# An RWKV-7, attention and expert encoder: the triangular inverse starts on its matrices, output products come in halves, opening rows go to ScalarE

## The chip, the cores and the metric

The kernel runs as one program on one core of a Trainium2 chip. The time is the device time of one execution in microseconds (us). A core has TensorE (PE; its weight loads are listed apart as PEld), VectorE (DVE), ScalarE (ACT), GpSimd (POOL) and SyncE (SP), which here only issues DMAs. Each engine works through its own instructions in order and waits on semaphores for the others.

## What is computed

One batch of 256 tokens with 1024 channels goes through two layers. Layer 0 mixes tokens with a bidirectional RWKV-7 recurrence, layer 1 with dilated window attention; behind each stands a mixture of 32 experts, of which every token takes two. The reference, cut to the part in which the change lies:

```python
for i in range(DEPTH):                       # DEPTH = 2
    mod = silu_c @ ada_w[i] + ada_b[i]       # six rows of 1024: shift, scale, gate, twice
    sh_t, sc_t, ga_t, sh_c, sc_c, ga_c = jnp.split(mod, N_MOD, axis=-1)
    hn = modulate(rms_norm(x, norm_tm_g[i]), sh_t, sc_t)
    tm = rwkv7_mix(hn, ...) if i % 2 == 0 else dilated_attention_mix(hn, ...)
    x = x + ga_t[:, None, :] * tm
    x = x + ga_c[:, None, :] * hier_moe(modulate(rms_norm(x, norm_cm_g[i]), sh_c, sc_c), ...)

def step(state, inp):                        # in rwkv7_mix, per head of 64, forwards and backwards
    sa = jnp.einsum('bhvk,bhk->bhv', state, a_t)
    state = state * w_t[:, :, None, :] + sa[:, :, :, None] * b_t[:, :, None, :] \
            + v_t[:, :, :, None] * k_t[:, :, None, :]
    y_t = jnp.einsum('bhvk,bhk->bhv', state, r_t)
# then: y normalised per head, gated by g, summed over both directions, and o @ w_o
```

## The kernel before, in words

The program has four stages, each of which needs the whole result of the one before: RWKV mixing, experts of layer 0, attention, experts of layer 1. The change touches the first alone.

**The opening.** `ada_rows` (line 402) forms the scale and shift rows of layer 0. For m = 1, then m = 0, 16 products with `silu` as weights (tile `row` in PSUM, two banks of 512 columns) add up over the eight slices of `w_ada`, which land in the ring `aring`. Each bank is copied to SBUF (`row[0]` by ScalarE, line 420; `row[1]` by VectorE, line 421), and eight products with the column `four` (tile `ada`) turn the 1024 values into eight columns; `ada_columns` (line 367) adds the bias and leaves them in `modc`. `scales` (line 481) and `modulated` (lines 674 to 684) use them on `xk`, `xr`, `xw`, `xa` and `xv`, of which `xk` feeds the first key products, tile `kr`.

**Eight pairs of heads.** Each pair i runs through four generators. `project` forms keys (`kr`), values (`v`), norms (`ss`, `vc`) and rates (`L`). `ready` (scale_keys, then chunks) scales the keys, forms the products `G`, masks them into `GV` and `GI` (line 927), casts the matrix to 16 bits (`Ah` on ScalarE at line 938, the rest `Al` on GpSimd at 939, minus the identity at 940), and goes on to the transposes `BT`, the products `R2` and the bonus `sT`; it then notes ("ready", i). `inverse` inverts the triangular matrix by doubling: each level is a round of small products (tile `iv`), an eviction `T` and `X` by ScalarE (line 999) and a masked `Q` by VectorE (line 1021); it ends with `TT` (line 1053). `recur` steps through four chunks (`U`, `S`, `Y`, `R1`), each step a product, an eviction and the next product. `finish` normalises the pair's output (`gvar` at line 1147, a reciprocal root of nine small VectorE instructions, `YT` at 1158), transposes it (`yT`) and gates it (`gT`).

**The order.** `weave` (line 277) writes the instructions of all generators into one order before anything runs: a generator yields a delay or a condition, a clock of estimated PE time (`pe_work`) decides whose turn it is, and `RANK` breaks ties. TensorE keeps this order as written; the other engines take theirs from the priorities that `weave` sets. Beside the pairs, `modulation_flow` adds up the other modulation rows on VectorE (line 376, tile `acc`) and ends each with eight products of one column (`ada<-cst,acc`), read by `modc` at line 367. `outputs` multiplies finished pairs with the output weights: `out_first` (pairs 0 to 3) and `out_second` (pairs 4 to 7), in blocks of 512 columns (tile `wo`). The last four blocks (pair 7) come behind the weave, then the router.

The condition that holds the inverse back before the change, and the one on its stream:

```python
            yield after(("ready", i))      # inverse, line 1005
            yield 1.0
                yield after(("ready", i))  # inverses, line 1303
```

Of the kernel before, what the change touches and what calls it, by code (L numbers as in the profile page):

```python
# [14 lines left out]
AF = mybir.ActivationFunctionType  # L15
# [219 lines left out]
def trunk(ctx, tc, names, aps, out, stages=("rwkv", "moe0", "attn", "moe1"), dbg=None, ring=2):  # L235
# [12 lines left out]
    def bank(name="ps", tag="ps"):  # L248
        return psum[-1][tag].tile([128, 512], F32, name=name, tag=tag)
# [11 lines left out]
    def on_pe(i):  # L261

        return tc.keep_in_program_order(i) if pinned[0] else i

    def mm(o, lhsT, rhs, start=True, stop=True, **kw):
        n = int(np.prod(rhs.shape[1:]))
        t = 2 * max(0.1, n / 1200) if rhs.dtype == F32 else max(0.03, n / 2400)
        if lhsT.shape[0] <= 64 or int(np.prod(lhsT.shape[1:])) <= 64:
            t /= 2
        pe_work[0] += t  # L270
        return on_pe(nc.tensor.matmul(out=o, lhsT=lhsT, rhs=rhs, start=start, stop=stop, **kw))  # L271
# [31 lines left out]
    V, A, P = nc.vector, nc.scalar, nc.gpsimd  # L303
# [98 lines left out]
    def ada_rows(tags, places, pool):  # L402


        four = pool.tile([128, 1], F32, name="four")
        V.tensor_reduce(out=four, in_=IDENT[:, 0:128:32], axis=AX.X, op=ALU.add)
        pc = bank(name="ada", tag=tags[4])
        for n, m in enumerate((1, 0)):
            ps = [bank(name="row", tag=t) for t in tags[2 * n:2 * n + 2]]
            for q in range(2):  # L410
                ws = modulations.take(*[(0, m, 4 * q + g) for g in range(4)])
                if modulations.issued >= len(ADA_FIRST):
                    stream.fill()
                for e in range(2):
                    for g in range(4):
                        k = 4 * q + g
                        mm(ps[e][32 * g:32 * g + 32, :], silu[:, k:k + 1].to_broadcast([128, 32]),
                           ws[g][:, e * 512:(e + 1) * 512], start=(q == 0), stop=(q == 1), skip_group_check=True)
            row = [p.tile([128, 512], F32, name="row", tag=t) for p, t in places[2 * n:2 * n + 2]]
            A.activation(out=row[0], in_=ps[0], func=AF.Copy)  # L420
            V.tensor_copy(out=row[1], in_=ps[1])
            for c in range(8):
                mm(pc[:, 8 * m + c:8 * m + c + 1], row[c // 4][:, c % 4 * 128:(c % 4 + 1) * 128], four)
            ada_columns(0, m, pc[:, 8 * m:8 * m + 8])
# [182 lines left out]
    def rwkv(pool):  # L607
# [137 lines left out]
        done = set()  # L745

        def after(*what):
            return lambda: all(w in done for w in what if w[1] >= 0)
# [165 lines left out]
        def chunks(i, w):  # L914

            AR, BK = w["AR"], w["BK"]
            GI = turns(i, [128, 2, 2, 4, 64], "GI")
            GV = sup.tile([128, 2, 2, 4, 64], F32, name="GV", bufs=1)
            aq = "p (a q) n -> p a q n"
            for z in range(2):  # L920
                pair = [bank(name="G") for _ in range(2)]
                for c in range(4):
                    for hh, ps in enumerate(pair):
                        mm(ps[:, c * 128:(c + 1) * 128], BK[half(hh), z, c, :], AR[half(hh), z, c, :])
                for hh, ps in enumerate(pair):
                    for o, t in ((0, GV), (64, GI)):
                        V.tensor_tensor(out=t[:, z, hh].rearrange(aq, q=2),
                                        in0=ps.rearrange("p (a q n) -> p a q n", a=2, q=2)[:, :, :, o:o + 64],
                                        in1=mk[:, z, :, o:o + 64].unsqueeze(1).to_broadcast([128, 2, 2, 64]),
                                        op=ALU.mult)  # L930
                yield 1.6

            gv = GV.rearrange("p z h c n -> p (z h) c n")
            Ah, Al = A16[2 * (i % 2):2 * (i % 2) + 2]
            for q in range(2):
                a = gv[half(q), :, 1 - q::2, :]
                h, l = (t.rearrange("p (g a) m -> p g a m", a=2)[half(q)] for t in (Ah, Al))
                A.copy(out=h, in_=a)
                P.tensor_tensor(out=l, in0=a, in1=h, op=ALU.subtract)
            V.tensor_tensor(out=Ah, in0=Ah, in1=N16.unsqueeze(1).to_broadcast([128, 8, 64]), op=ALU.add)  # L940
            if i == 0:
                yield lambda: "hidden_gate" in done
            BT = turns(i, [128, 2, 2, 2, 128], "BT")
            for par in range(2):
                ps = bank(name="BT")
                for z in range(2):
                    for a in range(2):
                        o = (z * 2 + a) * 128
                        tr(ps[:, o:o + 128], BK[:, z, 2 * a + par, :])
                A.activation(out=BT[:, par].rearrange("p z a n -> p (z a n)"), in_=ps, func=AF.Copy,  # L950
                             scale=sgn[:, par:par + 1])
                yield 0.1
            if i == 0:
                yield lambda: ("project", 0) in done
            vc = w["vc"]

            UV = turns(i, [128, 2, 4, 128], "UV")
            for z in range(2):
                for par in range(2):
                    A.copy(out=UV[half(par), z, par::2, :], in_=vc[half(par)])  # L960
            yield 0.1
            R2 = turns(i, [128, 4, 2, 64], "R2")
            ps = bank(name="R2")
            for s in range(4):
                for hh in range(2):
                    o = (s * 2 + hh) * 64
                    for z in range(2):
                        c = step_of(z, s)
                        p = half(c % 2)
                        mm(ps[half(1 - c % 2), o:o + 64], GV[p, z, hh, c, :], vc[p, c // 2, hh * 64:hh * 64 + 64])  # L970
            A.activation(out=R2.rearrange("p s h n -> p (s h n)"), in_=ps, func=AF.Copy)
            w.update(GI=GI, BT=BT, R2=R2, UV=UV)
            bonus(i, w)
            done.add(("ready", i))

        def inverse(i, w):
# [25 lines left out]
            def square():  # L1002
                return bank(name="iv", tag="iv")

            yield after(("ready", i))
            yield 1.0
            Ah, Al = A16[2 * (i % 2):2 * (i % 2) + 2]

            X = tile16("X16")
# [3 lines left out]
            for l in range(1, 6):  # L1013
# [4 lines left out]
                ps = square()  # L1018
# [14 lines left out]
            ps = square()  # L1033
# [22 lines left out]

        def recur(i, w):

            yield after(("inverse", i), ("finish", i - 2))
            yield 0.9  # L1060
            AR, GI, BT, TT, R2, UV, WC = (w[n] for n in ("AR", "GI", "BT", "TT", "R2", "UV", "WC"))
            YT = w["YT"] = sub.tile([128, 2, 2, 128], F32, name="YT")
# [1 line left out]
            for s in range(4):  # L1064
# [3 lines left out]
                else:  # L1068
                    R = odd.tile([128, 2, 64], F32, name="R", bufs=2)
                    ps = bank(name="R1", tag="ch")  # L1070
# [5 lines left out]
                ps = bank(name="U", tag="ch")  # L1076
# [8 lines left out]
                if s < 3:  # L1085
# [5 lines left out]
                    for z, c in enumerate(cz):  # L1091
                        for h, n in hs:
                            mm(pS[h, z * 64:z * 64 + 64], BT[:, c % 2, z, c // 2, n], UV[:, z, c, n],
                               start=(s == 0 and z == 0), stop=True, skip_group_check=True)
# [10 lines left out]
                if s > 0:  # L1105
                    for z, h in enumerate(hs):
                        mm(py[h, 0:128], AR[:, z, cz[z], 64:128], ST[:, z, :], start=True, stop=False,
                           skip_group_check=True)
                for hh in range(2):
                    for z, h in enumerate(hs):  # L1110
                        w["last"] = mm(py[h, hh * 64:hh * 64 + 64], GI[:, z, hh, cz[z], :], UV[:, z, cz[z], hh * 64:hh * 64 + 64],
                                       start=(s == 0 and hh == 0), stop=True, skip_group_check=True)
# [119 lines left out]
        def block(ps, t, w, k, start, stop):  # L1232
            mm(ps, oT[:, k, t * 128:(t + 1) * 128], w[:, (k % 4) * 512:(k % 4 + 1) * 512], start=start, stop=stop)

        def out_first():

            yield after(("project", 7), ("finish", 3), ("gate", 2))
            for c in range(2):
                w = gated(stream.take(("rwo", 0, c)), gates[0, 2][:, c * 512:(c + 1) * 512], 4)
                yield 6.0  # L1240
                for t in range(NTT):
                    ps = bank(name="wo", tag="pp")
                    for k in range(4):
                        block(ps, t, w, k, k == 0, k == 3)
                        yield
                    add_out(ps, t, c)

        def out_second(po, ks, w):
            for k in ks:
                for n, (t, c) in enumerate(po):  # L1250
                    if k == 6 and n == 2:
                        yield after(("recur", 7))
                    mm(po[t, c], oT[:, k, t * 128:(t + 1) * 128], w[:, k % 2, c * 512:(c + 1) * 512],
                       start=(k == 4), stop=(k == 7))
                    yield

        po, oT = {}, None

# [41 lines left out]

        def inverses():
            for i in range(8):
                yield after(("ready", i))
                yield from inverse(i, ws[i])

        def recurrences():
            for i in range(8):
                yield after(("inverse", i))
                yield from recur(i, ws[i])

        def finishes():
# [787 lines left out]
```

## Time and profile before

| | us |
|---|---|
| median of three runs | 1184.85 (1182.29 to 1189.32) |
| the profiled execution | 1175.46 |
| its span, first to last instruction | 1173.7 |
| PE busy in the span | 1031.4 (88%) |
| DVE busy | 620.2 (53%) |
| ACT busy | 431.6 (37%) |

The profile is of one execution. Its page gives the busy time of each engine, the span in 40 slices with the clock that TensorE was granted, the chain of work that ended last, and the costliest groups. Behind the page, the trace can be asked for instructions in order of time, for busy times in chosen stretches, and for who waited for whom. A number in brackets behind an instruction is the time that its engine sat idle just before it, with what ended that.

### The profile page before, as it was taken

The page shows a single profiled execution, that of the slowest core. Times are in us where ns is not written, and L with a number is a line of the kernel's source. Part 1 is how long each engine was busy: PE and PEld are TensorE (multiplying, and loading weights), DVE is VectorE, ACT ScalarE, POOL GpSimd, SP SyncE. Part 2 cuts the span into 40 slices and gives each one's busy share as a digit, 9 for nine tenths or more (in the row PEclk, how much of TensorE's full clock was granted, in tenths as well). Part 3 has the DMA queues.
Part 4 walks back from the last instruction along what each step waited for, and adds up shares of the span by engine and source line. Part 5 has one row for each costly group of instructions (what it writes and reads, how often), then busy time and mean ns, then how long its engine had stood idle before and what let it go on. Part 6 is the DMA issues. An engine that isn't in the chain of part 4 may idle for free. (4 is left out here: it accounts for less than half of the span.)

```text
span 1173.7 us, 25024 instructions
## 1 busy us (share of the span) xinstructions
PE 1031.4 (88%) x10580; PEld 675.4 (58%) x10580; DVE 620.2 (53%) x1460; ACT 431.6 (37%) x913; POOL 149.7 (13%) x110
## 2 busy tenths in 40 slices
PE   7789889999988998978987899898979999789886
PEld 2666667766766555434442388687868754344422
DVE  4774678478585446212211367999984752121112
ACT  2544455455446342101000366656544621010012
POOL 1020010010012600000000012122472000000000
PEclk9789999899979999989998999999989999899999
DMA  9462524325243676998999987887745589999995
GB/s 366 179 237 77 181 77 151 109 95 168 74 131 129 269 288 251 388 418 358 421 420 421 420 358 266 310 303 275 282 145 171 209 339 409 413 370 421 420 422 234
DMA packets 53197, 322.01 MB, mean 274 GB/s; under 512 B 5922, under 2 KB 6562, under 8 KB 21458
## 3 DMA queue, kind: packets, MB, share of 16 engines
q1 hardware_dynamic: 51986, 315.88, 69.0%
q0 software_dynamic: 800, 3.36, 0.7%
q8 instruction: 87, 1.43, 0.5%
q10 hardware_dynamic: 288, 1.05, 0.3%
q14 instruction: 36, 0.29, 0.1%
HBM read 319.22 MB, written 1.05 MB: 273 GB/s over the span
## 5 line engine op out<-in xcount | busy, mean ns | idle before, releaser
L271 PE MATMUL gu<-wring,xT 128*32 128x512 f32 x1024 | 132.6, 616 | 16.8 <-PEq L1609 10.2
L376 DVE SCALAR_TENSOR_TENSOR acc<-aring,silu,acc 128x512 f32<-128x512 f32 x140 | 116.0, 860 | 17.5 <-DMA aring<-in_w_ada_dram 17.3
L467 POOL TENSOR_TENSOR wl<-wring,wh 128x1024 f16<-128x1024 f32 x24 | 57.0, 2377 | 403.4 <-ACT wh L466 400.9
L271 PE MATMUL qkv<-hh,wh 128*128 128x256 f16 x384 | 106.1, 276 | 1.8 <-ACT hh L1761 1.8
L271 PE MATMUL qkv<-hl,wh 128*128 128x256 f16 x384 | 105.7, 276 | 1.8 <-DVE hl L1762 1.8
L271 PE MATMUL qkv<-hh,wl 128*128 128x256 f16 x384 | 106.0, 276 | 1.2 <-DVE wl L473 1.2
L271 PEld LDWEIGHTS gu<-wring,xT 128*32 128x32 f32 x1024 | 30.8, 112 | 100.5 <-issue 82.0
L271 PEld LDWEIGHTS <-wh 128*128 128x128 f16 x768 | 76.1, 99 | 12.8 <-issue 3.5
L271 PE MATMUL dn<-wring,hidT 128*32 128x256 f32 x1024 | 65.5, 404 | 18.4 <-ACT hidT L1564 18.4
L473 DVE SCALAR_TENSOR_TENSOR wl<-wring,wh 128x1024 f16<-128x1024 f32 x56 | 70.5, 1264 | 16.4 <-ACT wh L469 16.3
L271 PE MATMUL acc<-y,back 128*128 128x512 f32 (+1 forms) x144 | 66.0, 581 | 10.3 <-DVE y L1591 8.1
L271 PEld LDWEIGHTS xT<-oh,x 128*128 128x128 f32 x512 | 59.0, 192 | 21.1 <-issue 9.2
L469 ACT ACTIVATE wh<-wring 128x1024 f16<-128x1024 f32 x56 | 58.6, 1050 | 33.0 <-PE qkv L271 23.2
L1366 DVE SCALAR_TENSOR_TENSOR sg<-sg,gu 128x256 f32<-128x256 f32 x16 | 6.7, 420 | 116.8 <-ACT sg L1365 116.8
L1591 DVE TENSOR_TENSOR y<-dn,ga 128x512 f32<-128x512 f32 x28 | 19.4, 692 | 88.3 <-PE dn L271 56.7
L271 PE MATMUL xT<-oh,x 128*128 128x128 f32 x512 | 63.5, 280 | 2.5 <-DVE oh L1475 2.5
L1365 ACT ACTIVATE sg<-gu 128x256 f32<-128x256 f32 x16 | 6.1, 384 | 145.6 <-PE gu L271 145.6
L271 PEld LDWEIGHTS dn<-wring,hidT 128*32 128x32 f32 x1024 | 31.9, 115 | 48.2 <-ACT hidT L1564 22.3
L1507 ACT ACTIVATE back<-bT 128x256 f32<-128x256 f32 x16 | 6.2, 386 | 131.0 <-PE acc L271 131.0
L271 PE MATMUL qkv<-wh,hh 128*128 128x256 f16 x192 | 52.3, 273 | 0.0
L271 PE MATMUL qkv<-wh,hl 128*128 128x256 f16 x192 | 52.3, 273 | 0.0
L271 PE MATMUL qkv<-wl,hh 128*128 128x256 f16 x192 | 52.3, 273 | 0.0
(355 smaller groups left out, 2090.4 us busy)
## 6 DMA issues: line engine op xcount, KB each, us to landing
wring<-in_w_moe_dram SPq DMA_DIRECT2D x192, 1024.0 KB, 19.8
aring<-in_w_ada_dram SPq DMA_DIRECT2D x96, 512.0 KB, 4.6
wring<-in_w_qkv_dram SPq DMA_DIRECT2D x36, 1024.0 KB, 8.4
wring<-in_w_kr_dram SPq DMA_DIRECT2D x8, 1024.0 KB, 5.9
wring<-in_w_vl_dram SPq DMA_DIRECT2D x8, 640.0 KB, 5.0
wring<-in_w_rwo_dram SPq DMA_DIRECT2D x4, 1024.0 KB, 8.1
wring<-in_w_ato_dram SPq DMA_DIRECT2D x4, 1024.0 KB, 6.6
x<-in_x_dram POOLq DMA_DIRECT2D x2, 512.0 KB, 7.2
```

The costliest lines, as they stand in the source:

```text
L271: return on_pe(nc.tensor.matmul(out=o, lhsT=lhsT, rhs=rhs, start=start, stop=stop, **kw))
L376: V.scalar_tensor_tensor(out=acc[:, s], in0=w[:, s], scalar=silu[:, k:k + 1], in1=acc[:, s], op0=ALU.mult, op1=ALU.add)
L467: eng.tensor_tensor(out=lo, in0=src, in1=hi, op=ALU.subtract)
L469: A.activation(out=hi, in_=src, func=AF.Copy, scale=by)
L473: V.scalar_tensor_tensor(out=lo, in0=src, scalar=by, in1=hi, op0=ALU.mult, op1=ALU.subtract)
L1365: A.activation(out=o, in_=ps[:, 0:256], func=AF.Tanh, scale=0.5)
L1366: V.scalar_tensor_tensor(out=o, in0=o, scalar=1.0, in1=ps[:, 0:256], op0=ALU.add, op1=ALU.mult)
L1507: A.activation(out=back, in_=ps[:, 0:S], func=AF.Copy)
L1591: V.tensor_tensor(out=y, in0=py[c], in1=gates[i, 5][:, c * 512:(c + 1) * 512], op=ALU.mult)
```

## The change

Three edits. First, `chunks` notes ("matrices", i) as soon as `Ah` is complete, and `inverse` waits for that in place of ("ready", i), then 4.0 of the planner's units in place of 1.0; `recur` now asks for ("ready", i) itself. Second, the output products are written as two products of 256 columns, with a yield behind each. Third, the second bank of the opening rows is copied by ScalarE.

```diff
@@ ada_rows
             A.activation(out=row[0], in_=ps[0], func=AF.Copy)
-            V.tensor_copy(out=row[1], in_=ps[1])
+            A.activation(out=row[1], in_=ps[1], func=AF.Copy)
@@ chunks
             V.tensor_tensor(out=Ah, in0=Ah, in1=N16.unsqueeze(1).to_broadcast([128, 8, 64]), op=ALU.add)
+            done.add(("matrices", i))
@@ inverse
-            yield after(("ready", i))
-            yield 1.0
+            yield after(("matrices", i))
+            yield 4.0
@@ recur
-            yield after(("inverse", i), ("finish", i - 2))
+            yield after(("inverse", i), ("ready", i), ("finish", i - 2))
@@ out_first
-                        block(ps, t, w, k, k == 0, k == 3)
-                        yield
+                        for e in range(2):
+                            o = slice(e * 256, e * 256 + 256)
+                            mm(ps[:, o], oT[:, k, t * 128:(t + 1) * 128], w[:, k * 512 + e * 256:k * 512 + e * 256 + 256],
+                               start=(k == 0 and e == 0), stop=(k == 3), skip_group_check=True)
+                            yield
@@ out_second
-                    mm(po[t, c], oT[:, k, t * 128:(t + 1) * 128], w[:, k % 2, c * 512:(c + 1) * 512],
-                       start=(k == 4), stop=(k == 7))
-                    yield
+                    for e in range(2):
+                        o = c * 512 + e * 256
+                        mm(po[t, c][:, e * 256:e * 256 + 256], oT[:, k, t * 128:(t + 1) * 128], w[:, k % 2, o:o + 256],
+                           start=(k == 4 and e == 0), stop=(k == 7), skip_group_check=True)
+                        yield
@@ inverses, recurrences
-                yield after(("ready", i))
+                yield after(("matrices", i))
-                yield after(("inverse", i))
+                yield after(("inverse", i), ("ready", i))
```

What this does to the order shows at three places. First VectorE in the opening, behind the mixes of `pGI`; - is before, + is now.

```order
 L645 SCALAR_TENSOR_TENSOR pGI<-xx,muh,hT 128x256 x8
-L421 COPY row<-row 128x512 x2
 L367 TENSOR_TENSOR modc<-ada,cols 128x8
 L645 SCALAR_TENSOR_TENSOR xv<-xx,muh,hT 128x256
-L367 TENSOR_TENSOR modc<-ada,cols 128x8
 L481 TENSOR_SCALAR nsc<-modc 128x8
 L645 SCALAR_TENSOR_TENSOR xv<-xx,muh,hT 128x256
 L482 TENSOR_TENSOR nsc<-nsc,cols 128x8
-L675 SCALAR_TENSOR_TENSOR end<-muh,modc 128x8 x2
+L645 SCALAR_TENSOR_TENSOR xv<-xx,muh,hT 128x256
+L367 TENSOR_TENSOR modc<-ada,cols 128x8
+L645 SCALAR_TENSOR_TENSOR xv<-xx,muh,hT 128x256
```

The two copies are gone from VectorE, and the second `modc` stands two mixes of `xv` later.

Second, TensorE behind the products `G` of pair 0 (`hg` are the gate's hidden products). Before:

```order
L271 MATMUL G<-AR,BK 128x128 x16
L271 MATMUL hg<-pBT,wring 128x256 x16
L275 MATMUL BT<-cst,BK 128x128 x4
L271 MATMUL kr<-xk,wring 128x256 x2
L275 MATMUL BT<-cst,BK 128x128 x4
L271 MATMUL kr<-xk,wring 128x256 x4
L271 MATMUL R_689<-vc,GV 64x64 x16
L271 MATMUL sT<-bb,cstr 128x256 x2
```

Now:

```order
L271 MATMUL vc<-cstr,vT 128x128 x2
L271 MATMUL G<-AR,BK 128x128 x16
L271 MATMUL hg<-pBT,wring 128x256 x8
L271 LDWEIGHTS X_640
L271 MATMUL iv<-cst_324,X_640 64x64
```

The inverse of pair 0 begins behind eight of the sixteen `hg` products, where before it came behind all of them, the transposes, `R2`, `sT` and some keys.

Third, VectorE where pair 4 is normalised (`gvar` to `YT`), beside a modulation row whose `modc` waits for one-column products on TensorE. Before:

```order
L1021 TENSOR_TENSOR Q_4615<-iv,cst_324 128x512
L1147 TENSOR_REDUCE gvar<-gsq 128x8
L367 TENSOR_TENSOR modc<-ada,cols 128x8
L1148 TENSOR_SCALAR gvar<-gvar 128x8
L374 TENSOR_SCALAR acc<-aring,silu 128x512
L345 TENSOR_SCALAR rsy<-gvar 128x8
L347 TENSOR_SCALAR rsh<-gvar 128x8
L795 TENSOR_SCALAR kss<-ss 128x4
L348 TENSOR_TENSOR rsq<-rsy 128x8
```

Now:

```order
L367 TENSOR_TENSOR modc<-ada,cols 128x8
L374 TENSOR_SCALAR acc<-aring,silu 128x512 x2
L376 SCALAR_TENSOR_TENSOR acc<-aring,silu,acc 128x512
L1022 TENSOR_TENSOR Q_4626<-iv,cst_324 128x512
L1148 TENSOR_REDUCE gvar<-gsq 128x8
L376 SCALAR_TENSOR_TENSOR acc<-aring,silu,acc 128x512
L1149 TENSOR_SCALAR gvar<-gvar 128x8
L1750 TENSOR_SCALAR nsh<-modc 128x8
L345 TENSOR_SCALAR rsy<-gvar 128x8
```

`modc` and the first sums of the next row moved ahead of `gvar`, and `kss`, the start of another reciprocal root, left this stretch.

## Rows read from the trace of the kernel before

**Rows 1.** The page's granted clock, in tenths, over 40 slices.

```profile
PEclk9789999899979999989998999999989999899999
```

**Rows 2.** Busy us (and instructions) per engine by stretch; then clock, DMA share, GB/s.

```profile
72.29:454.84 382.55, 349.37 (x5171) 253.75 (x5172) 240.81 (x616) 181.48 (x409) 56.88 (x46) 0.94 0.42 150
...
469.05:535.00 65.95, 55.25 (x468) 27.50 (x472) 15.76 (x41) 9.04 (x25) 0.00 (x0) 0.95 0.92 374
535.00:660.00 125.00, 110.34 (x866) 46.28 (x862) 20.93 (x49) 11.71 (x33) 0.00 (x0) 0.96 1.01 421
...
530.00:532.00 2.00, 2.00 (x21) 2.00 (x20) 1.27 (x5) 0.00 (x0) 0.00 (x0) 1.00 0.12 49
```

**Rows 3.** Instructions in order of time, opening: start, duration, engine, what, idle before.

```profile
22.86 9.33 PE L271 MATMUL row<-aring,silu 128*32 128x512 f32 x32
...
31.36 0.60 ACT L420 ACTIVATE row<-row 128x512 f32<-128x512 f32 x1 [9.64 <-PE row L271]
32.00 3.25 DVE L645 SCALAR_TENSOR_TENSOR pGI<-xx,muh,hT 128x256 f32<-128x256 f32 x8
...
35.16 1.28 DVE L421 COPY row<-row 128x512 f32<-128x512 f32 x2
...
38.12 3.54 PE L271 MATMUL ada<-four,row 128*128 128x1 f32 x16 [0.35 <-DVE modc L367]
38.32 0.48 DVE L645 SCALAR_TENSOR_TENSOR xv<-xx,muh,hT 128x256 f32<-128x256 f32 x1 [0.35 <-DMA cstr<-in_k_cst_dram]
41.70 0.17 DVE L367 TENSOR_TENSOR modc<-ada,cols 128x8 f32<-128x8 f32 x1 [2.89 <-PE ada L271]
...
42.48 1.38 DVE L680 TENSOR_SCALAR xk<-pUV,nsc,modc 128x256 f32<-128x256 f32 x4
...
44.03 6.07 PE L271 MATMUL kr<-xk,wring 128*128 128x256 f32 x16 [2.38 <-issue]
```

**Rows 4.** Busy times and clock, two microseconds in the opening, columns as in Rows 2.

```profile
46.00:48.00 2.00, 2.00 (x6) 1.56 (x5) 2.00 (x10) 2.00 (x5) 0.00 (x0) 0.50 0.00 0
```

**Rows 5.** In order of time, pair 0 behind its G products.

```profile
77.76 8.05 PE L271 MATMUL hg<-pBT,wring 128*128 128x256 f32 x32
...
83.17 0.42 DVE L1010 TENSOR_TENSOR X<-Ah,cst 128x512 f16<-128x512 f16 x1
...
93.07 0.44 PE L271 MATMUL iv<-cst,X 64*64 64x64 f16 x16
```

**Rows 6.** In order of time, TensorE and VectorE where pairs 3 and 4 are normalised.

```profile
278.85 0.50 PE L271 MATMUL ss<-cstr,ksq 128*128 128x2 f32 x4
...
284.49 1.08 PE L275 MATMUL yT<-cst,YT 128*128 128x128 f32 x4 [1.70 <-DVE rsq L353]
...
295.61 1.27 PE L271 MATMUL G<-AR,BK 64*128 64x128 f32 x16 [0.91 <-DVE BK L887]
...
318.86 1.84 PE L271 MATMUL ada<-cst,acc 128*128 128x1 f32 x16
320.74 0.17 DVE L367 TENSOR_TENSOR modc<-ada,cols 128x8 f32<-128x8 f32 x1 [1.10 <-PE ada L271]
321.26 0.61 PE L271 MATMUL ss<-cstr,ksq 128*128 128x2 f32 x4
...
326.22 1.08 PE L275 MATMUL yT<-cst,YT 128*128 128x128 f32 x4 [2.89 <-DVE rsq L352]
...
343.81 1.31 PE L271 MATMUL G<-AR,BK 64*128 64x128 f32 x16
```

**Rows 7.** Busy times and clock inside that stretch of pair 4.

```profile
322.00:324.00 2.00, 1.33 (x20) 0.97 (x19) 2.00 (x11) 1.35 (x4) 0.00 (x0) 0.50 0.30 29
...
336.00:338.00 2.00, 2.00 (x35) 1.43 (x34) 2.00 (x5) 0.93 (x3) 0.00 (x0) 0.50 0.71 258
```

**Rows 8.** In order of time, products of 256 columns with their loads, and of 512.

```profile
50.16 3.43 PEld L271 LDWEIGHTS kr<-xr,wring 128*128 128x128 f32 x16
50.37 3.62 PE L271 MATMUL kr<-xr,wring 128*128 128x256 f32 x16
...
450.16 4.84 PE L271 MATMUL wo<-wring,oT 128*128 128x512 f32 x10
```

**Rows 9.** In order of time, TensorE in the first experts, third group of eight.

```profile
519.20 9.97 PE L271 MATMUL gu<-wring,xT 128*32 128x512 f32 x64 [5.11 <-PEq L1609]
```

## Prediction

> **What bounds the kernel now.** I read the stretches by stage first, then the opening and the pairs in order of time, then the places where TensorE waits. From the first `G` product at 72.29 us to the end of the output products at 454.84 TensorE is busy for 349.37 of 382.55 us [rows 2]: it is the bound there, and at most 33.2 us of waiting can be won. Two things sit inside that. The granted clock was 0.94 of full over the stretch [rows 2], so single parts of it ran at 0.50, which is 1.2 GHz in place of 2.4 [rows 7]; the page shows such dips all over the span [rows 1]. And single waits reach 2.89 us [rows 6]. Ahead of 72 us it is a chain: rows, their copies, `modc`, `xk`, first keys. TensorE begins the keys at 44.03 only [rows 3].
>
> What does a shorter first stage give to the end? From 535 to 660 the DMA engines move 421 GB/s at a share of 1.01, so the end of the first experts is set by DMA. But just before, at 530 to 532, the share is 0.12 [rows 2]: the buffers are full and the queue waits for TensorE, which came late because of a branch (5.11 us idle at 519.20) [rows 9]. TensorE alone paces 469 to 535 (no row of it waits for weights), so whatever the first stage ends earlier moves this point, and all that follows, by as much. I count 1 for 1.
>
> **The opening.** Before, VectorE mixes `pGI` until 35.25, copies both second halves from 35.16, waits for the columns until 41.70, and starts `xk` at 42.48; keys follow 1.55 us later at 44.03 [rows 3]. ScalarE had been idle for 9.64 us at 31.36 [rows 3], so the copies cost it nothing: two of 0.60 us. Now m = 0's last rows end at 32.19 (22.86 + 9.33), its second copy by 32.9, and eight columns behind it come by 34 to 35 even at the slower clock (3.54 us bought 16 pieces). VectorE leaves `pGI` at 35.25 and, in its new order, has four `xv` mixes, two `modc`, two `nsc` and one `end` ahead of `xk`. With full durations of 0.48 and 0.17, and the 0.35 us of idle seen ahead of the first `xv`, that is 3.0 us; with the spacing of back-to-back starts (about 0.40 and 0.09) it is 2.4. So `xk` starts at 37.7 to 38.3 and the keys at 39.2 to 39.8: **4.2 to 4.8 us earlier, I take 4.5**. The columns have some 2 us of cover there; were it gone, each late microsecond would cost one. The keys' own 6.07 us stay: they ran at 0.50 [rows 4] after an idle TensorE, and TensorE is idle ahead of them now too. Everything behind (rates, values, `G`) hangs on the keys and moves along.
>
> **The earlier inverse.** No work is removed. What can change is the waiting. Pair 0: `X` was ready at 83.59 while the inverse's first product stood at 93.07 [rows 5]. Now it stands behind half of the `hg` products, at 77.76 + 4.0 = 81.8 of the old time, so TensorE waits 1.8 us for VectorE, and `hg`, transposes and keys queue behind: **+1.8**. Later pairs: counted in the order, the inverse of pair 1 begins no earlier than before among TensorE's instructions, as its projection was pushed behind inverse 0; those of pairs 3 to 7 begin at most a few microseconds earlier. The steps of inverse and recurrence have as much other work between them as before (34 places before and 36 now with less than an eviction's time in between), so I take nothing there.
>
> Three places differ. Pair 3's `yT` waited 1.70 us for its reciprocal root [rows 6], which now stands on VectorE without another root or sums in between: **-1.7**. Pair 4's `yT` waited 2.89 us, partly since VectorE stood 1.10 us at `modc` for the one-column products [rows 6]; that is ahead of `gvar` now, though sums still stand in between: **-1.4**. New thin places are pair 1's `yT`, behind a recurrence that no inverse runs beside, and inverse 7, where fewer output products stand in between; the trace has no such place, so from below 0 is possible, from above 2.89, the longest wait of this kind; near to 1.70, I take 1.5 each: **+3.0**. Waits together: +1.8 - 1.7 - 1.4 + 3.0 = **+1.7**, bounds -3.1 (only what goes) to +7.6 (nothing goes, both new ones at 2.89).
>
> The clock: from `ss` to the next pair's `G` took 22.55 us at pair 4 (321.26 to 343.81) and 16.76 at pair 3 (278.85 to 295.61), with about the same work [rows 6]. Of the 5.8 us between them 1.2 are the longer wait, **4.6 are the half clock**, which held from 322 to past 336 [rows 7]. Ahead of it TensorE did one-column products (1.84 us at 318.86), `ss` and `vc`, and then idled. In the new order the one-column products stand half a pair earlier, away from `ss`, `vc` and the wait. Whether the clock then holds no row can tell; I take 0.6 of it, **-2.8**, with bounds -4.6 (it holds) and +4.6 (one more such stretch at a new thin place).
>
> **The halves.** 32 blocks become 64 of half the width. A run of ten pieces of 512 columns took 4.84 us, 0.48 each; sixteen of 256 took 3.62, 0.23 each, with the weight loads (3.43 us) running beside them [rows 8]. So two halves cost 0.46 against 0.48: 0. The runs into which the output products are cut by other work go from 23 to 25. Finer filling is in the counts above.
>
> That the loads run beside products of the same 128 rows is what rows 8 show. The Trainium skill ("TensorE: Matmul & The Clock Gate", part 3, what overlaps and what doesn't) says that a weight load overlaps a running product only if it goes to other row groups of the array. By that the halves' loads would be exposed, and the sum would come out above the time before; the rows here don't agree, and the case is the fourth rival.
>
> **Sum.** -4.5 + 1.7 - 2.8 + 0 = -5.6 us. Against the profiled execution (1175.46, span 1173.7 and 1.8 around it) that is 1169.9; the median of the runs lies 9.4 above that execution, and 1184.85 - 5.6 = **1179.2**.
>
> **Rivals.**
> 1. The opening alone, since the inverse is not really earlier behind pair 0: new waits of 4.8, none removed, clock as before: -4.5 + 4.8 = +0.3, 1185.2. For it: the order of pair 1. Against: the removed obstacles on VectorE are plain in the order.
> 2. The middle closes up: waits at their lower bound, the half clock at pair 4 gone: -4.5 - 3.1 - 4.6 = -12.2, 1172.6. For it: that stretch was unlike its neighbour. Against: other dips [rows 1] came without it.
> 3. Slower by the clock: each of the two thin places (pair 1's `yT`, inverse 7) brings a half-clock stretch like that of pair 4, 5.8 us each, and nothing else improves: -4.5 + 4.8 + 11.6 = +11.9, 1196.8. It decides from both stretches on; one alone leaves +6.1.
> 4. Slower by weight loads: 32 more products of two pieces are 64 loads of 0.21 us (3.43 / 16), 13.7 us if all were exposed: -5.6 + 13.7 = +8.1, 1193.0. It takes over 84% of them to lose 0.5%. Against it: rows 8.
>
> **How the numbers follow.** About 0.5% (5.9 us) is what a measurement of this kernel can tell from no change. The forecast, 1179.2 with its own range of 1175 to 1183, has 0.50, and lies at that line, so I split it evenly. Rival 1 has 0.15 (within), rival 2 has 0.23 (faster), rival 3 has 0.08 and rival 4 has 0.04 (slower). Faster 0.25 + 0.23 = 0.48, within 0.25 + 0.15 = 0.40, slower 0.12. The range reaches from rival 2's lower side, 1171, to above rival 1, 1189, and leaves rivals 3 and 4 out.
>
> **What would show it.** In the profile after: keys starting near 39.5; a wait of about 2 us ahead of the first `iv` product of pair 0; `yT` of pairs 3 and 4 with little idle before them, and pair 1's with 1 to 3; the clock in the slices of 320 to 340; half output products at 0.23 us a piece; the first `gu` at about 463. Wrong would be: keys starting later than 42, pieces of 0.3 us or more, or a DMA stall at 530 that no longer exists, so that DMA paces the first experts from their start and the gain is lost there.

## The result and the profile after

The changed kernel took **1193.11 us** in the median of 12 runs against 1187.51 for the kernel before: a ratio of **1.0059 (95% interval 1.0031 to 1.0087)**, some 7 us slower. (The medians are 5.6 us apart; the ratio is of the means and leaves out one execution of the changed kernel, of 3282 us.) The forecast was 1179.2, faster, with a range of 1171 to 1189. It was wrong in size and in sign.

The profiled execution of before that the prediction used (1175.46) was the shortest of all executions of that kernel, whose median is 1187 to 1188. I therefore profiled the kernel before once more (run `before_again`, 1190.97), and compare by stretches. Each number is the time between two of these points in the trace: the first `kr` product, the first `G` product, the first `ss` product of pair 7, the end of its last `G` product, the first `zT` product (the output's transposes; the output products are done), the first `gu` product.

| us | before | before again | after |
|---|---|---|---|
| first `kr` at | 44.0 | 44.6 | 41.5 |
| `kr` to first `G` | 28.3 | 29.8 | 29.6 |
| first `G` to `ss` of pair 7 | 298.1 | 300.8 | 296.5 |
| **`ss` of pair 7 to its last `G`** | 20.5 | 20.5 | **36.2** |
| last `G` to `zT` | 64.0 | 65.5 | 63.9 |
| `zT` to `gu` | 14.2 | 14.2 | 14.2 |
| first `gu` at | 469.1 | 475.3 | 481.9 |

Against `before_again` the parts up to `gu` come to -3.1 - 0.2 - 4.3 + 15.7 - 1.6 = +6.5, close to the 5.6 between the medians. The keys did start earlier; that the middle gained is not shown, since over nine profiles of kernels with the inverse as before it takes 294.9 to 301.3 us. One stretch of 20 us, of which the prediction never speaks, grew by 15.7. The busy times and the clock of the stretches, for before and then for after (columns as in [rows 2]):

```profile
72.29:370.35 298.06, 272.28 (x4109) 206.76 (x4109) 197.58 (x486) 145.49 (x324) 32.17 (x28) 0.93 0.36 118
370.35:390.86 20.51, 18.12 (x269) 13.76 (x263) 15.59 (x47) 11.26 (x24) 12.45 (x10) 0.83 0.80 326
```

```profile
71.09:367.58 296.49, 266.45 (x4124) 202.06 (x4125) 199.17 (x488) 147.54 (x330) 33.07 (x28) 0.97 0.37 123
367.58:403.81 36.23, 22.71 (x309) 18.28 (x306) 27.21 (x46) 10.88 (x23) 20.02 (x15) 0.67 0.47 175
403.81:467.73 63.92, 58.19 (x812) 44.04 (x812) 27.83 (x83) 24.35 (x61) 4.30 (x4) 1.00 0.63 247
```

In the middle line of after TensorE is idle for 13.5 us (36.23 - 22.71), before for 2.4; the other 4.6 us are TensorE's own, for 309 instructions in place of 269 and at a clock of 0.67 in place of 0.83. VectorE is busy 27.21 us with 46 instructions; before it needed 15.59 for 47. It does not do more: **it takes longer for the same**. In order of time, VectorE and TensorE of after in that stretch:

```profile
367.43 1.19 DVE L1149 TENSOR_SCALAR gvar<-gvar 128x8 f32<-128x8 f32 x1
368.65 1.19 DVE L345 TENSOR_SCALAR rsy<-gvar 128x8 int32<-128x8 int32 x1
369.75 0.16 DVE L347 TENSOR_SCALAR rsh<-gvar 128x8 f32<-128x8 f32 x1
369.87 1.18 DVE L348 TENSOR_TENSOR rsq<-rsy 128x8 f32<-128x8 f32 x1
371.09 1.19 DVE L349 TENSOR_TENSOR rsq<-rsq,gvar 128x8 f32<-128x8 f32 x1
372.93 0.64 PE L271 MATMUL iv<-Q,X 64*64 64x64 f16 x16 [4.19 <-DVE Q L1022]
...
385.19 0.68 DVE L1022 TENSOR_TENSOR Q<-iv,cst 128x512 f16<-128x512 f32 x1
...
392.36 1.48 DVE L887 TENSOR_TENSOR BK<-kd,e 128x256 f32<-128x256 f32 x1
393.77 1.48 DVE L887 TENSOR_TENSOR BK<-bb,e 128x256 f32<-128x256 f32 x1
395.17 1.48 DVE L887 TENSOR_TENSOR BK<-kd,e 128x256 f32<-128x256 f32 x1
395.30 0.80 PE L271 MATMUL G<-AR,BK 64*128 64x128 f32 x4 [6.78 <-DVE BK L887]
396.57 1.48 DVE L887 TENSOR_TENSOR BK<-bb,e 128x256 f32<-128x256 f32 x1
```

and GpSimd (POOL) at the same time, in after:

```profile
363.64 8.62 POOL L590 TENSOR_TENSOR wring<-wring,ga 128x512 f32<-128x512 f32 x7 [11.13 <-PE U L271]
382.43 1.39 POOL L1169 TENSOR_TENSOR yn<-yn,sT 128x512 f32<-128x512 f32 x1 [10.18 <-ACT yn L1167]
383.78 2.94 POOL L590 TENSOR_TENSOR wring<-wring,ga 128x512 f32<-128x512 f32 x2
386.69 0.73 POOL L1171 TENSOR_TENSOR oT<-yn 128x256 f32<-128x256 f32 x1
387.37 10.40 POOL L590 TENSOR_TENSOR wring<-wring,ga 128x512 f32<-128x512 f32 x7
```

Line 590 (`gated`) is untouched by the change: GpSimd multiplies the output weights `wring` by the gate `ga`, sixteen instructions in all. A `BK` alone takes 0.42 us; beside them it takes 1.48, one `BK` to each scaling. Instructions of 128x8 that took 0.16 to 0.17 before take 1.19 (`rsh` alone among the five kept its 0.16). `Q`, which reads one operand from PSUM (`iv`), keeps its 0.68 amid them (385.19). TensorE waits 4.19 us for `Q`, which stands behind part of the root on VectorE, and 6.78 and 2.01 for `BK`.

Before, GpSimd and VectorE had the same work, but not together:

```profile
366.66 4.95 POOL L590 TENSOR_TENSOR wring<-wring,ga 128x512 f32<-128x512 f32 x4 [12.94 <-PE R L271]
379.66 3.36 POOL L1168 TENSOR_TENSOR yn<-yn,sT 128x512 f32<-128x512 f32 x1 [8.06 <-ACT yn L1166]
382.98 7.85 POOL L590 TENSOR_TENSOR wring<-wring,ga 128x512 f32<-128x512 f32 x6
```

```profile
379.19 0.42 DVE L887 TENSOR_TENSOR BK<-bb,e 128x256 f32<-128x256 f32 x1
379.53 0.76 DVE L887 TENSOR_TENSOR BK<-kd,e 128x256 f32<-128x256 f32 x2
380.20 0.42 DVE L887 TENSOR_TENSOR BK<-bb,e 128x256 f32<-128x256 f32 x1
380.53 0.76 DVE L894 TENSOR_TENSOR AR<-kk,eb 128x256 f32<-128x256 f32 x2
381.20 0.69 DVE L895 TENSOR_TENSOR AR<-krT,eb 128x512 f32<-128x512 f32 x1
381.81 1.76 DVE L897 SCALAR_TENSOR_TENSOR bb<-krT,colr,kd 128x512 f32<-128x512 f32 x1
385.65 0.42 DVE L927 TENSOR_TENSOR GV<-G,cstr 128x256 f32<-128x256 f32 x1 [0.70 <-PE G L271]
```

From 371.6 to 379.7 GpSimd stood at `yn` of pair 5, waiting for ScalarE. In that gap VectorE did the reciprocal root and began pair 7's `BK`. The rest of `BK` and `AR` ran from 379.5 to 381.9 at full speed while GpSimd was in `yn`, which took long itself (3.36 us; last section); of VectorE's work only `bb` behind them is long (1.76, alone 0.69). So two of the expectations below, which put most of `BK` and `AR` into the gap, read these rows wrongly. When the scalings went on at 382.98, `BK` and `AR` were done; the masks `GV`, which read `G` from PSUM, kept their 0.42 beside them. The order of GpSimd's queue shows how the gap closed; it could be read ahead of any run. Before, then after (with the lines of each):

```
L590 TENSOR_TENSOR wring<-wring,ga_998 128x512 x4
L1168 TENSOR_TENSOR yn<-yn,sT 128x512
L590 TENSOR_TENSOR wring<-wring,ga_998 128x512 x6
L1170 TENSOR_TENSOR oT<-yn 128x256
L590 TENSOR_TENSOR wring<-wring,ga_998 128x512 x6

L590 TENSOR_TENSOR wring<-wring,ga_1170 128x512 x7
L1169 TENSOR_TENSOR yn<-yn,sT 128x512
L590 TENSOR_TENSOR wring<-wring,ga_1170 128x512 x2
L1171 TENSOR_TENSOR oT<-yn 128x256
L590 TENSOR_TENSOR wring<-wring,ga_1170 128x512 x7
```

The Trainium skill has this as a rule ("SBUF — State Buffer", section Who interferes with whom): a VectorE instruction with two inputs in SBUF, or in one of its two-port modes, shares a port pair with a GpSimd instruction that reads SBUF, and the one that comes second is blocked until the first ends; one with a single SBUF input outside those modes is not. The rows agree: `BK` at 1.48, `Q` at 0.68. They show durations, not the port.

### The profile page after: what moved, and what is told of

The parts are those of the page before. It is cut to its first block, busy times and chain, and to the rows that moved or that the text cites. A ratio compares the mean times of both kernels' runs of the same rounds, so it can differ in the third digit from the quotient of the medians.

```text
span 1190.7 us, 25143 instructions
## 1 busy us (share of the span) xinstructions
PE 1032.9 (87%) x10644; PEld 689.1 (58%) x10644; DVE 631.0 (53%) x1458; ACT 432.5 (36%) x915; POOL 148.5 (12%) x110
## 3 DMA queue, kind: packets, MB, share of 16 engines
q0 software_dynamic: 800, 3.36, 0.8%
```

## The experiments

The theories: **A**, the scalings beside VectorE make the loss; **B**, the thin places and the clock (rival 3); **C**, the weight loads of the halves (rival 4). D to H came up on the way. All ratios are to runs of before on the same chip, from ten runs of each kernel (inverse alone four; copy, inverse, gate on products six; the change twelve). The stretches, in us, are each from one profile; before and before again differ by 1.5 in the last of them (64.0 and 65.5).

| kernel | ratio (95%) | `ss` 7 to last `G` | last `G` to `zT` |
|---|---|---|---|
| copy alone | 0.9967 (0.9936 to 0.9998) | 20.5 | 65.5 |
| inverse alone | 1.0145 (1.0090 to 1.0199) | 37.1 | 65.6 |
| halves alone | 1.0057 (1.0021 to 1.0093) | 20.1 | 73.6 |
| copy and inverse | 1.0075 (1.0044 to 1.0106) | 37.0 | 65.6 |
| copy and halves | 1.0024 (0.9995 to 1.0052) | 20.1 | 74.0 |
| all three (the change) | 1.0059 (1.0031 to 1.0087) | 36.2 | 63.9 |
| the change, gate on products | 0.9987 (0.9955 to 1.0019) | 20.0 | 67.2 |
| the change, second gate on products | 0.9993 (0.9967 to 1.0020) | 26.4 | 65.5 |
| before, gate on products | 0.9966 (0.9933 to 0.9999) | 20.5 | 62.1 |
| copy, gate on products | 0.9943 (0.9911 to 0.9974) | 20.5 | 62.1 |
| copy, inverse, gate on products | 0.9944 (0.9918 to 0.9969) | 19.5 | 65.9 |
| before, made to collide | 1.0037 (1.0008 to 1.0066) | 31.1 | 61.9 |
| halves with one yield | 0.9985 (0.9955 to 1.0015) | 20.5 | 65.3 |

**The three parts alone**, each put into the kernel before: only the line of the copy; only the five lines of the earlier inverse; only the two loops over halves.

```diff
-            V.tensor_copy(out=row[1], in_=ps[1])
+            A.activation(out=row[1], in_=ps[1], func=AF.Copy)
```

> The kernel before with only the ScalarE copy of the second opening bank. All theories agree on it: keys (kr) start about 2.5 us earlier, as in the changed kernel (41.50 against 44.03), the G products of pair 0 start 1 to 2.5 us earlier, and the time falls by 1 to 3 us (ratio 0.997 to 0.999). If the opening were what costs the change its gain, the ratio would be above 1.000.

```diff
-            yield after(("ready", i))
-            yield 1.0
+            yield after(("matrices", i))
+            yield 4.0
```

> The kernel before with only the earlier inverse. Theory A (GpSimd's sixteen scalings of the output weights, line 590, run at the same time as VectorE's work with two operands in SBUF and hold it up at pair 7): all of the loss is here, 7 to 12 us (ratio 1.006 to 1.010); the stretch from ss of pair 7 to its last G product takes over 10 us longer than the 20.5 us of before, with BK and AR instructions of 128x256 at 1.4 to 1.5 us in place of 0.42, and the loss is nowhere else. Theory B (thin places: waits at pair 1's yT and at inverse 7, and the half clock behind them): 7 to 12 us too, but spread over the pairs, with the VectorE instructions at their usual length.

```diff
-                        block(ps, t, w, k, k == 0, k == 3)
-                        yield
+                        for e in range(2):
+                            ...
+                            yield
```

> The kernel before with only the output products in halves. Theories A and B: within 2 us of before (ratio 0.998 to 1.002), wo products of 256 columns spaced 0.23 us a piece. Theory C (the weight loads of the halves are exposed): 8 to 13 us slower (ratio 1.007 to 1.011).

The copy brings 0.33% (3.9 us), a little over the 1 to 3 us expected and near the prediction's 4.5. The inverse alone costs 1.45%, more than the whole change and more than the 0.6 to 1.0% that A expected, and all of it that shows lies in the one stretch (37.1 us); from the first `G` to `ss` of pair 7 it took 298.1 us, as before. `BK` and `AR` are at 1.48. That is A and not B. The halves alone cost 0.57%, which A and B did not expect, but not as C has it: their stretch from the last `G` on is 8 to 10 us longer, at a granted clock of 0.88 (before 1.00, before again 0.97; columns as in [rows 2]).

```profile
391.40:465.00 73.60, 65.95 (x863) 49.37 (x864) 27.43 (x83) 24.95 (x62) 12.64 (x12) 0.88 0.59 227
```

**The halves without the finer order**: two products a block, but one yield.

```diff
                         for e in range(2):
                             ...
-                            yield
+                        yield
```

> The kernel before with the output products in halves, but one yield for the two halves of a block, so that the order is that of before with each block written as two products. Theory C (the halves themselves cost, by their weight loads): as the halves alone, ratio 1.004 to 1.008. Theory F (it is the finer order: half as much between two steps, more left for the end, and the half clock behind the waits): back at before, ratio 0.998 to 1.002.

Back at before: the halves themselves (224 `wo` pieces in the trace in place of 160, each with its weight load) cost nothing that shows, and it is the order. The same stretch of this kernel:

```profile
395.00:460.20 65.20, 59.44 (x861) 44.64 (x861) 27.62 (x83) 24.74 (x62) 12.21 (x11) 1.00 0.61 236
```

In the finer order a free place gets one half where it got a whole block, so that more is left for the end. The last output products, halves alone first, then halves with one yield:

```profile
451.45 4.42 PE L271 MATMUL wo<-wring,oT 128*128 128x256 f32 x18
...
455.92 9.23 PE L271 MATMUL wo<-wring,oT 128*128 128x256 f32 x42
```

```profile
451.30 3.72 PE L271 MATMUL wo<-wring,oT 128*128 128x256 f32 x16
...
455.50 4.86 PE L271 MATMUL wo<-wring,oT 128*128 128x256 f32 x20
```

Sixty pieces at the end against 36, and TensorE is idle for 7.7 us in the stretch against 5.8 (73.60 - 65.95 and 65.20 - 59.44), with an estimated 17.7 us at the half clock ((1 - 0.88) x 73.6 x 2). At full clock, by the same estimate, the 73.6 us would be some 65. That the larger rest at the end is what brings the waits and the half clock is argued, not shown.

**One part left out**, the halves and then the inverse (the diffs above, reversed).

> The changed kernel without the halves. Theory D (halves fill the gaps between the steps with half as much and leave more for the end, and cost this in any order): 4 to 8 us below the changed kernel, ratio 0.999 to 1.002. Theory E (what the halves cost or bring depends on the rest): since the inverse alone stands at 1.0145 and the copy alone at 0.9967, 1.010 to 1.013, that is 4 to 8 us above the changed kernel.

> The changed kernel without the earlier inverse. If the parts add up, the copy (0.9967) and the halves (1.0057) give 1.001 to 1.004, 2 to 6 us below the changed kernel, with the loss of the halves in the tail: from the last G product to the output's transposes over 70 us, against 64 to 65.5 of before. If the halves' cost hangs on the rest, as it does beside the earlier inverse (63.9 us), 0.996 to 0.999.

Without the halves the kernel is not faster (1.0075 against 1.0059, within each other's intervals), which lies between the ranges of D and E and bears out neither. Without the inverse the parts add up (1.0024; tail 74.0 us, clock 0.88 again). So the halves' cost is there where the inverse is late, and doesn't show in the changed kernel, whose tail takes 63.9 us at full clock. Why the clock holds there I can't say; with the scalings gone it falls to 0.95 in the tail of the same order (67.2 us).

**The scalings taken away**: the gate is multiplied into the products in PSUM.

```diff
-                w = gated(stream.take(("rwo", 0, c)), gates[0, 2][:, c * 512:(c + 1) * 512], 4)
+                w = stream.take(("rwo", 0, c))
...
+                    gate_out(ps, c)
                     add_out(ps, t, c)
...
+        def gate_out(ps, c):
+            V.tensor_tensor(out=ps, in0=ps, in1=gates[0, 2][:, c * 512:(c + 1) * 512], op=ALU.mult)
```

> The changed kernel with the gate multiplied into the output products in PSUM (eight VectorE instructions of 128x512, about 0.7 us each, four of them behind the last product, some 1.5 us on the path) in place of GpSimd's sixteen scalings of the weights. Theory A: the stretch from ss of pair 7 to its last G product falls from 36 us to 20 to 23, BK and AR are back at 0.42 us, and the time falls 8 to 14 us below the changed kernel, to a ratio of 0.993 to 0.999 against before. Theory B: it stays at the changed kernel's 1.005 to 1.008, since the thin places are as before.

As A has it: the stretch is at 20.0 us, and 8.5 us (0.72%) come back. That is less than the 16.2 us that the stretch lost: in the profiles the tail is 3.3 us longer at its lower clock, and the four multiplications behind the last product take 0.7 (`zT` to `gu` 14.9 in place of 14.2). Its row of windows, and VectorE in it:

```profile
364.65:384.64 19.99, 17.52 (x309) 14.14 (x306) 14.82 (x46) 10.90 (x23) 2.28 (x2) 0.91 0.78 291
```

```profile
378.97 0.41 DVE L887 TENSOR_TENSOR BK<-kd,e 128x256 f32<-128x256 f32 x1
379.31 0.41 DVE L887 TENSOR_TENSOR BK<-bb,e 128x256 f32<-128x256 f32 x1
```

The same 46 instructions of VectorE take 14.82 us in place of 27.21, and TensorE's same 309 take 17.52 in place of 22.71.

**Half of the dose**: the gate on the products for pairs 4 to 7 alone. (The expectation names pair 6's root; it is pair 5's.)

> The changed kernel with the gate on the products for the second half of the pairs alone; the scalings of the first half (eight of the sixteen) stay on GpSimd, seven of them where the reciprocal root of pair 6 runs, while the seven that met BK and AR of pair 7 are gone. Theory A: BK and AR at 0.42 us, the three long instructions of the reciprocal root (1.18 us) remain, so some 9 of the 13 us of lengthening go: 4 to 7 us below the changed kernel, ratio 0.999 to 1.003, between it and the kernel with no scalings (0.9987). Theory G (any scaling there costs the whole, by an idle TensorE and its clock): as the changed kernel, 1.004 to 1.008.

The stretch falls between (26.4 us), `BK` is at 0.42 and four instructions of the root at 0.88 to 1.31. The time fell by as much as with no scalings, within the intervals. Against G, for A.

**The same in the kernel before.**

> The kernel before with the gate multiplied into the output products in place of GpSimd's sixteen scalings. Before, VectorE's BK and AR of pair 7 ran at 0.42 us, in a gap of GpSimd's work (371.6 to 379.7 us). Theory A (it is the change that makes the scalings collide): nothing to win here, the eight multiplications add 0 to 2 us, ratio 0.998 to 1.002. Theory A2 (the scalings cost the kernel before as much): 6 to 9 us faster, ratio 0.992 to 0.995.

It gains 0.34%, between A and A2, and not in the stretch (20.5 both). In the profile the tail is 2 to 3 us shorter: before, GpSimd reached `Al` of pair 7 only behind the last six scalings, at 398.82, and VectorE stood at it:

```profile
401.23 0.43 DVE L940 TENSOR_TENSOR Ah<-Ah,cst 128x512 f16<-128x512 f16 x1 [8.91 <-POOL Al L939]
...
402.84 1.12 PE L271 MATMUL wo<-wring,oT 128*128 128x512 f32 x2 [1.83 <-DVE x L596]
```

Without scalings the wait for `Al` is 2.82 us, and `x` at line 596 comes in time.

**The collision made in the kernel before**, with no part of the change: GpSimd no longer stops at `yn`.

```diff
-            P.tensor_tensor(out=y, in0=y, in1=sT, op=ALU.add)
+            E = V if i == 5 else P
+            E.tensor_tensor(out=y, in0=y, in1=sT, op=ALU.add)
...
-            P.tensor_tensor(out=oT[:, i], in0=y[:, 0:S], in1=y[:, S:2 * S], op=ALU.add)
+            E.tensor_tensor(out=oT[:, i], in0=y[:, 0:S], in1=y[:, S:2 * S], op=ALU.add)
```

> The kernel before, with nothing of the change, but the two additions of pair 5's normalisation (yn and oT) on VectorE in place of GpSimd, 1.1 us of work. Before, GpSimd stood from 371.6 to 379.7 us at the first of them, and VectorE did a reciprocal root and most of pair 7's BK and AR in that gap; now the sixteen scalings run without a gap. Theory A (scalings beside VectorE's work with two operands in SBUF make the loss): that work is lengthened to 1.2 to 1.5 us an instruction, the stretch from ss of pair 7 to its last G product grows from 20.5 us to 30 to 38, 8 to 16 us slower, ratio 1.007 to 1.013, with TensorE's and VectorE's order otherwise that of before. Rival H (the earlier inverse itself makes the stretch long, the scalings are a bystander): 20 to 22 us, ratio 0.999 to 1.002.

```profile
369.20 4.96 POOL L590 TENSOR_TENSOR wring<-wring,ga 128x512 f32<-128x512 f32 x4 [13.06 <-PE R L271]
381.05 17.84 POOL L590 TENSOR_TENSOR wring<-wring,ga 128x512 f32<-128x512 f32 x12 [6.89 <-PE iv L271]
```

```profile
383.03 2.89 DVE L887 TENSOR_TENSOR BK<-kd,e 128x256 f32<-128x256 f32 x2
387.24 2.88 DVE L894 TENSOR_TENSOR AR<-kk,eb 128x256 f32<-128x256 f32 x2
391.71 1.75 DVE L897 SCALAR_TENSOR_TENSOR bb<-krT,colr,kd 128x512 f32<-128x512 f32 x1
```

The stretch grows to 31.1 us with TensorE's order unchanged, and VectorE's but for the two additions and one mask: the scalings are enough, and H falls. But the time rose by 0.37% only, not by the 0.7 to 1.3% I expected. In the profile the tail gave 2 to 3.5 us back (61.9 us; it is as short in the kernels of before and copy without scalings, where `Al` isn't late either), and the keys began 2 us earlier, at 42.2, with the columns ahead of them partly at full clock (16 pieces in 2.91 us, in [rows 3] 3.54); the edit doesn't touch them.

**Without the collision, is the earlier inverse worth anything?**

> The changed kernel without the halves and with the gate on the products. Theory A: the collision is gone here as in the kernel with halves, 8 to 14 us below the kernel of copy and inverse. Theory D: 3 to 7 us below the same kernel with halves, ratio 0.993 to 0.996. Theory E: above it, 1.000 to 1.004.

> The kernel before with the ScalarE copy and the gate on the products, the inverse and the blocks as before. Theory A: the copy's gain alone, ratio 0.995 to 0.999. If the earlier inverse is worth something once the collision is out of the way, the kernel of copy, inverse and gate is faster than this one by over 3 us; if it is worth nothing, they are within 3 us.

Nothing that shows: 0.9944 and 0.9943, each to 0.3%. (The second is a little below the 0.995 to 0.999 expected; taking the scalings out of the kernel before gave 0.34% as well.) Both beat the kernel before and the changed one; the simpler is the copy with the gate on the products, the order left as it was. Once the collision is gone the halves seem to cost some 0.4% again (0.9987 against 0.9944), as D has it, though the intervals overlap.

**A second profile of before.**

> The kernel before, unchanged, for a second profile: the profiled execution of before (1175.46) lies 12 us below the median of its runs. If TensorE's clock makes the difference, the second profile has the same VectorE durations at pair 7 (BK at 0.42) and more stretches at 0.50.

`BK` is at 0.42 again, the stretch at 20.5 us, the mean clock at 0.943 against 0.951. Over 25 runs of before the mean clock went from 0.953 (1181.80 us) to 0.938 (1193.75 us), with a correlation of -0.76 between clock and time: much of the difference between executions, not all of it, goes with how often TensorE was at the half clock. Of the 15.5 us between the two spans, 6.3 fall ahead of the first `gu` and 9.2 behind it.

## Why the prediction was wrong, step by step

- **The missing step.** For the later pairs I counted TensorE's order, found as much other work between the steps as before, and took nothing. I did not look at GpSimd's queue, which the earlier inverse also re-sorts (4, 6, 6 scalings became 7, 2, 7; so too in the kernels of inverse alone and of copy and inverse, while copy alone and halves alone keep 4, 6, 6), nor ask with what on VectorE these coincide. VectorE's instructions I took at their old durations; beside the scalings they took 1.19 for 0.16 and 1.48 for 0.42, and TensorE, for which I had put no new wait there, waited 13 us for them. That is 15.7 us in the profile, and 1.3% between the kernel of copy and inverse with the scalings (1.0075) and without (0.9944).
- **The opening, -4.5.** Right by time: the copy alone gave 0.33%, 3.9 us. The keys, forecast for 39.5, began at 41.50 in the changed kernel's profile. The cover that I named was not there: TensorE's columns for m = 0 started only when VectorE had read those of m = 1, and ran at the half clock in 3.39 us. Of the eight profiles with the copy, four have the columns at or near full clock (copy alone 1.92 us) and keys at 38.9 to 39.4, and four are like this one:

```profile
35.96 3.39 PE L271 MATMUL ada<-four,row 128*128 128x1 f32 x16 [3.59 <-DVE modc L367]
39.39 0.17 DVE L367 TENSOR_TENSOR modc<-ada,cols 128x8 f32<-128x8 f32 x1 [2.23 <-PE ada L271]
```

- **The waits, +1.7.** The size is right apart from the collision, the places only in part. From the first `G` to `ss` of pair 7 TensorE is idle for 25.8 us before (27.6 before again) and 30.0 after, the rows above say: +2.4 to +4.3, within the bounds. Pair 0's first `iv` product waited 2.47 (forecast 1.8), pair 1's `yT` 2.73 (1.5, at most 2.89), pairs 3 and 4's `yT` 0.42 and 0.19 (forecast 0 and 1.5). Missed were pair 1's first `iv` product and pair 2's `yT`:

```profile
81.76 0.44 PE L271 MATMUL iv<-cst,X 64*64 64x64 f16 x16 [2.47 <-DVE X L1011]
141.82 0.41 PE L271 MATMUL iv<-cst,X 64*64 64x64 f16 x10 [3.72 <-DVE X L1011]
243.61 0.63 PE L275 MATMUL yT<-cst,YT 128*128 128x128 f32 x4 [1.47 <-DVE rsy L351]
```

- **The clock, -2.8.** In its place right, even undersized: the 22.55 us of [rows 6] beside the normalisation of pair 4 (the `ss` and the `G` are pair 6's) became 17.0, with TensorE idle no less (3.9 us, before 3.3). Before, then after:

```profile
321.26:343.81 22.55, 19.21 (x232) 13.37 (x227) 18.49 (x51) 10.13 (x21) 2.43 (x2) 0.62 0.54 169
...
326.00:343.00 17.00, 13.11 (x212) 9.47 (x214) 14.40 (x37) 9.95 (x21) 2.50 (x2) 1.00 0.49 167
```

  In four of the six kernels with the earlier inverse the clock there was still 0.73, and the stretch took 19. And half clocks came elsewhere: at pair 7 (0.67), behind TensorE's new waits, and behind pair 1's `yT`.
- **The halves, 0.** Right for their price (halves with one yield: 0.9985; the rule of the fourth rival is not borne out), wrong for their order where it acts without the earlier inverse; in the changed kernel it cost nothing that shows.
- **1 for 1 behind the first stage.** Right. Over the 15 profiles a first `gu` later by 1 us goes with a span longer by 1.0 us (a fitted line, `gu` from 464.7 to 489.7), though what stands behind it varies from 704.6, in the profile of before that I used, to 719.1. First `gu` 12.85 us later than in [rows 9]'s profile, and the group behind the branch 12.89 later (532.09 against 519.20), with the DMA queue nearly idle at one place behind it (share 0.04), as in [rows 2]:

```profile
532.09 9.93 PE L271 MATMUL gu<-wring,xT 128*32 128x512 f32 x64 [5.13 <-PEq L1615]
...
544.00:546.00 2.00, 2.00 (x21) 1.99 (x19) 1.37 (x4) 0.11 (x1) 0.00 (x0) 1.00 0.04 16
```

- **The rivals.** Rival 1 (the earlier inverse is not worth anything) is what is left once the collision is gone. Rival 2 fell (pair 3 and 4's waits went as it says, but others came). Rival 3 had the right sign for a reason that did not occur: of its two thin places pair 1's `yT` waited as long as feared and was followed by a half clock of some 6 us (204 to 210, clock 0.50), inverse 7's products waited 0.75 us at most. Rival 4 fell with the halves of one yield (0.9985).

## What to carry to other kernels

Where a planner or priorities set the order, an edit on one engine re-sorts all the queues: read the new order of the engine that seems idle too, and ask for each stretch on the path whether GpSimd now reads SBUF beside VectorE's work with two operands there. An instruction's duration belongs to what runs beside it; a wait on GpSimd that looks like waste, as `yn` of pair 5, may be what keeps two engines apart. And a finer grain of filling isn't always free: it fills each gap with less, and cost 0.57% alone.

## What the runs showed of the hardware

- Small instructions pay as much as large ones: beside the scalings a VectorE instruction of 128x8 went from 0.16 to 1.19 us, one of 128x256 from 0.42 to 1.48, each longer by 1.0 to 1.1 (a scaling alone takes 1.23). GpSimd pays less (10.40 us for seven scalings, 1.49 each, against 7.38 for six, 1.23 each, beside the masks).
- It is not always VectorE that waits. Before, `yn` on GpSimd came while VectorE was at `BK`, and took 3.36 us in place of 1.26, while four `BK` and three `AR` ran at their full speed. What decides between this and the taking of turns seen in after, no run here shows.
